# Gated attention heads finished in pairs: values, row sums and gates in groups, with the order of two projection tiles and of the gate matmuls changed

## The chip, the cores and the metric

The kernel runs on one core of one Trainium2 chip. The metric is the device time of one execution in microseconds. Before the change the median of three runs is 1924.27 us (1922.54 to 1924.54).

## What is computed

The reference is a two-layer encoder trunk on 512 tokens of width 1024:

```
for l in range(2):
    x = x + 0.5 * swiglu(rmsnorm(x))                   # feed-forward, 1024 -> 2816 -> 1024
    proj = rmsnorm(x) @ w_in                           # q,k,v | gq,gk,gv,gr | two gate codes
    na  = rmsnorm(neighbourhood_attention(q, k, v))    # 8 heads of 64
    gla = rmsnorm(o_fwd + o_bwd) * silu(gr)            # 4 gated linear-attention heads, dv = 128
    x = x + concat(na, gla) @ w_out
    x = x + 0.5 * swiglu(rmsnorm(x))
return rmsnorm(x)
```

A gated head has queries and keys of 64 and values of 128. Its forget gate comes from a rank-16 code, `log_sigmoid(code @ w_gate + b) / 16`, once for each direction. The head's output is divided by its root mean square, multiplied by a gain and by `silu(gr)`.

## The kernel before

All data is float32. Large products are made of three matmuls on float32r halves (`mm3`, line 182): the high part of the weights with both parts of the input, the low part with the high part. Between the two feed-forward stages of a layer stands `mixer` (line 583). It is the stage that the change touches; it runs twice.

The mixer has four streams of work, each a Python generator: the two pairs of gated heads (`gla_all(0)`, `gla_all(1)`, line 1036), the neighbourhood attention (`na_all`, line 969), and the filler (`fillers`, line 997), which makes the projection tiles of `win` in the order of `PAIRS` (line 39) and then multiplies by `w_out`. `interleave` (line 529) decides the order in which the streams are written. Each generator yields a pair (cost, delay): the planner adds the cost to its own clock and lets the stream go on no sooner than the delay after that. A yield of a name waits until the name stands in `got`. In each round the planner lets all streams that are due take steps in the order pair 0, neighbourhood attention, pair 1; then it runs what the last round left in `pend` (the transposes of gated values, line 772); then it takes filler steps for 5.3 units (`SLOT`). A filler step of a projection tile is six matmuls at 1.36 units.

TensorE's instructions are pinned to the order of writing while `interleave` runs (line 120). The orders of ScalarE and VectorE are chosen at compile time by a scheduler that plays the program through; they then run strictly in that order, each instruction waiting for its inputs.

PSUM has eight banks: four of tag `mm`, two of tag `sc`, one `tp` and one `o`. A bank can be written again only when every reader of its last content is done.

The parts that the change touches:

- `gla_gates` (line 611) makes the two gate tiles of a pair, one for each direction `d`. A gate tile is two matmuls into a bank, a ScalarE Abs and a VectorE minimum (line 622) that read the bank, and a chain after them. Pair 0 uses the `sc` banks; pair 1 uses `o` for the first direction and `tp` for the second, one directly behind the other.
- `gla_out` (line 797) ends one head. It waits for the head's `silu(gr)` (name `gs`) and transposed values (`gv`), issues 16 matmuls into an `mm` bank, squares and copies the result on ScalarE, and yields 3.6. Then `rsqrt_ms` (line 245) sums the squares over the partitions by two matmuls into `tp` (first head of a pair) or `sc` (second head). The row is read from the bank by two ScalarE instructions, Ln (line 261) and Identity (line 264); Exp (line 262) and three VectorE instructions follow. Two products on VectorE and `osplit` (line 794) give the parts `oh` that the output product needs.
- `rsqrt_ms` is also called once for the neighbourhood heads (line 989), into `tp`. The transposes of the attention probabilities (line 948) and of the gated values go through `tp` too.
- The filler's last part waits for the outputs of the heads, multiplies the neighbourhood half of `w_out` (eight chunks, `op_part(c, 0, 4)`) and half of the gated half for four chunks. What is left (`op_part(c, 6, 2)` and `op_part(c, 4, 4)`, line 1058) is done behind `interleave`; the profile calls that stage OP. Its weights come through two raw buffers and six split buffers.

In the rows, names that begin with M_ are tiles of the mixer, OP_ of the output stage, F_ of the feed-forward; M_sqh and M_sql are the two halves of a row sum's input, M_gr the gate value, M_gv the transposed values, M_pp the attention probabilities, M_mn the minimum of line 622, M_am the copies of the 128-wide scores.

Of the kernel before, what the change touches and what calls it, by code (L numbers as in the profile page):

```python
# [9 lines left out]
F32 = mybir.dt.float32  # L10
F32R = mybir.dt.float32r
U8 = mybir.dt.uint8
AF = mybir.ActivationFunctionType
ALU = mybir.AluOpType

P = 128
# [10 lines left out]
FAL = 1.4  # L27
HEAD = 9
MMB = 4
GOT = ('mm', 'mm')  # L30
WARM = 13
NAP = 4.0
SLOT = 5.3
# [10 lines left out]
         ('gk1', 'gq1'),  # L44
         ('q3', 'k3'),
         ('v2', 'v3'),
         ('gr0', 'gr1'),
         ('gv2', 'gv3'),
         ('gv0', 'gv1'),
         ('gr2', 'gr3'))  # L50
COLS = {"q": 0, "k": 512, "v": 1024, "gq": 1536, "gk": 1792, "gv": 2048, "gr": 2560}
TAGS = {'sl': 12, 'g0': 8, 'g1': 8, 'na': 6, 'ws': 5}
NPR = 12
NDF = 3
OPT = 2.56
OUTT = 3.6
GOTT = ('g0', 'g1')
# [3 lines left out]
def trunk_kernel(ctx, tc, xin, wgu, wdn, win, wcode, wgate, wout, vec, rpbt,  # L61
                 lmask, onesid, out, depth=DEPTH, stop=None):
    nc = tc.nc
    V, S, G, PE = nc.vector, nc.scalar, nc.gpsimd, nc.tensor
# [25 lines left out]
    def lvec(l, i):  # L90
        o = voff + l * 9 + i
        return vecs[:, o:o + 1]
# [4 lines left out]
    def nm(s):  # L97
        cnt[0] += 1
        return f"{st['lab']}_{s}_{cnt[0]}"

    def sl(name="s", dt=F32, tag="sl"):
        return sp.tile([P, T], dt, tag=tag, name=nm(name), bufs=TAGS[tag])

# [10 lines left out]
    def psum(tag):  # L114
        pool = {"mm": pm, "sc": ps2}.get(tag, ps1)
        return pool.tile([P, T], F32, tag=tag, name=nm(tag))

    def pinned(ins):

        if st.get("pin"):  # L120
            tc.keep_in_program_order(ins)
        return ins

    def MM(*args, **kw):
        return pinned(PE.matmul(*args, **kw))  # L125
# [30 lines left out]
    def split(src, h, l, gain=None):  # L156
        if gain is None:
            S.activation(h, src, AF.Copy)  # L158
            V.tensor_tensor(l, src, h.bitcast(F32), op=ALU.subtract)  # L159
        else:  # L160
            S.activation(h, src, AF.Copy, scale=gain)
            V.scalar_tensor_tensor(l, src, gain, h.bitcast(F32), ALU.mult, ALU.subtract)
# [79 lines left out]
    def lnexp():  # L242
        tc.keep_in_program_order(S.preload_act_table_set("natural_log_exp_and_others"))

    def rsqrt_ms(src, n, load=False, tag="sl", bank="tp"):
        if load:
            lnexp()
        ps = psum(bank)
        if tag == "sl":
            MM(ps, ones, src, start=True, stop=True)  # L250
        else:
            h, l = sl("sqh", F32R, tag), sl("sql", F32R, tag)
            split(src, h, l)
            MM(ps, onr, h, start=True, stop=False)
            MM(ps, onr, l, start=False, stop=True)

        return rsqrt_row(ps, n, *(sl(k, F32, tag) for k in ("ms", "r", "a")), act=tag != "sl")

    def rsqrt_row(ps, n, t, r, a, act=False):

        S.activation(r, ps, AF.Ln, bias=epsc, scale=1.0 / n)
        S.activation(r, r, AF.Exp, scale=-0.5)
        if act:
            S.activation(t, ps, AF.Identity, bias=epsc, scale=1.0 / n)
        else:
            V.tensor_scalar(t, ps, 1.0 / n, EPS, ALU.mult, ALU.add)
        V.tensor_tensor(a, r, r, op=ALU.mult)
        V.scalar_tensor_tensor(a, a, -0.5, t, ALU.mult, ALU.mult)  # L268
        V.scalar_tensor_tensor(r, a, 1.5, r, ALU.add, ALU.mult)
        return r  # L270
# [306 lines left out]
    def seq_out(a):  # L577
        return a.rearrange("p (r u c) -> p u r c", r=8, u=8)

    def unit_in(a):  # L580
        return a.rearrange("p (u r c) -> p u r c", u=8, r=8)

    def mixer(l):
        st["lab"] = f"M{l}"
        got = {}
# [23 lines left out]
        gla = [{}, {}]  # L609

        def gla_gates(pr):
            g = gla[pr]
            for d in range(2):
                gs, pk = sl("gs", F32, f"g{pr}"), sl("pk", F32, f"g{pr}")
                pg = psum("sc" if pr == 0 else ("o", "tp")[d])
                cs = slice(d * 256 + pr * P, d * 256 + (pr + 1) * P)
                MM(pg, wgh[:, cs], cr, start=True, stop=False)
                MM(pg, wgl[:64, cs], cr[:64], start=False, stop=True)
                b = lvec(l, 5 + 2 * d + pr)
                ab, mn = sl("ab", F32, "ws"), sl("mn", F32, "ws")  # L620
                S.activation(ab, pg, AF.Abs, bias=b)
                V.tensor_scalar(mn, pg, b, 0.0, ALU.add, ALU.min)
                S.activation(ab, ab, AF.Exp, scale=-1.0)
                S.activation(ab, ab, AF.Ln, bias=1.0)
                V.tensor_tensor(gs, mn, ab, op=ALU.subtract)
                prev = gs
                for h in (2, 4, 8, 16, 32, 64, 128):
                    n = T // h
                    cur = pk[:, GOFF[h]:GOFF[h] + n]
                    pv = prev.rearrange("p (b two) -> p two b", two=2)  # L630
                    V.tensor_tensor(cur, pv[:, 0, :], pv[:, 1, :], op=ALU.add)
                    prev = cur
                S.activation(gs, gs, AF.Exp, scale=1.0 / 16.0)
                S.activation(pk[:, :508], pk[:, :508], AF.Exp, scale=1.0 / 16.0)
                g["t1", d], g["tp", d] = gs, pk
# [11 lines left out]

        def gla_levels(pr):
            g = gla[pr]
            gla_gates(pr)  # L650
            yield 1.8, 6.0
            yield ("gq", pr)
            qa, ka = got["gq", pr], got["gk", pr]
# [5 lines left out]
            at = g["at"] = []  # L659
# [35 lines left out]
            for li, h in enumerate((1, 2, 4, 8, 16, 32, 64, 128)):  # L695
# [45 lines left out]
                elif h2 == 128:  # L741
                    pss = psum("sc"), psum("sc")
                    mms = []
                    for s in range(4):
                        t = s ^ 1
# [8 lines left out]
                else:  # L754
                    for half in range(2):
                        pss = psum("sc"), psum("sc")
                        kk, qq = (KF, QF) if half == 0 else (KB, QB)
                        o = 256 * (1 - half)
# [35 lines left out]
        def osplit(src, k, gain):  # L794
            ohl[k] = pair("oh", gain, src)

        def gla_out(hd, tag):
            g = gla[hd // 2]
            hh = hd % 2
            yield ("gs", hd)  # L800
            yield ("gv", hd)
            po = psum(tag)
            v = got["gv", hd]

            def vs(s):
                return v[:, s * P:(s + 1) * P]

            for t in range(4):
                dst = po[:, t * P:(t + 1) * P]
                half = 1 - t // 2  # L810
                fa = g["f", hh, half]
                s1 = t ^ 1
                MM(dst, vs(t), g["at"][hh][:, t * P:(t + 1) * P], start=True, stop=False)
                MM(dst, vs(s1), g["m", hh][:, s1 * P:(s1 + 1) * P], start=False, stop=False)
                for j in range(2):
                    o = j * 256 + (t % 2) * P
                    MM(dst, vs(2 * half + j), fa[:, o:o + P], start=False, stop=(j == 1))
            tag = GOTT[hd // 2]
            on, sq = sl("on", F32, tag), sl("sq", F32, tag)
            S.activation(sq, po, AF.Square)  # L820
            S.activation(on, po, AF.Copy, scale=0.125)
            got["po", hd] = True
            yield OUTT, 1.0
            r = rsqrt_ms(sq, 64 * P, False, tag, ("tp", "sc")[hh])
            V.tensor_tensor(on, on, r, op=ALU.mult)
            gp = got["gr", hd]
            V.tensor_tensor(unit_in(gp), seq_out(on), unit_in(gp), op=ALU.mult)
            osplit(gp, 4 + hd, lvec(l, 4))
            got["oh", hd] = True
            yield 0.9, 0.0  # L830


        def vmat_steps(src, done):
# [163 lines left out]
        def fillers():  # L997
            for i, (a, b) in enumerate(PAIRS):
                if i == 0:
                    continue  # L1000

                def done(j, ps):
                    turn = posts[a](j, ps, st["s"])
                    if turn:
                        pend.append(turn)

                steps = vmat_steps if a in ("v0", "v2") else tile_steps
                yield from steps(win[l, i], done)

            yield ("na",)  # L1010
            for c in range(KD):
                op_part(c, 0, 4)
                o = sl("on", F32, "ws")
                V.tensor_tensor(o, pss[c], got["na"], op=ALU.mult)  # L1014
                V.tensor_tensor(xt[:, c, :], xt[:, c, :], o, op=ALU.add)
                yield OPT, 0.0
            for hd in (1, 3):
                yield ("po", hd)
            yield ("oh", 0)
            yield ("oh", 1)  # L1020
            for c in range(MMB):
                op_part(c, 4, 2)
                yield 1.28, 0.0
# [11 lines left out]

        def gla_all(pr):
            yield from gla_levels(pr)
            for hd in (2 * pr, 2 * pr + 1):
                yield from gla_out(hd, GOT[pr])

        raw, ws = st.pop("dpre", (None, None))
        b0 = dmat(win[l, 0], ("mm", "mm"), raw, ws)
        r = stage_row()
# [25 lines left out]
    for c in range(KD):  # L1069
        xsplit(c, 0)  # L1070
        if c % 2 == 0:
            h, l = wnew()
# [147 lines left out]
```

## Time and profile before

| what | value |
|---|---|
| median of three runs | 1924.27 us |
| the profiled execution's own time | 1924.05 us |
| its span in the trace | 1922.3 us |
| VectorE busy | 1407.5 us (73%) |
| ScalarE busy | 1034.9 us (54%) |
| 16 DMA engines | 98 GB/s on average |
| chain that ended last | TensorE 91%, VectorE 4%, ScalarE 3% |

The time outside the span is 1.75 us. A busy TensorE means that a matmul is in the array; an instruction that waits at the head of its queue shows as idle time with the one that released it in brackets. Matmuls overlap by about half a duration, so issue distances are read from start to start.

### The profile page before, as it was taken

The page shows a single profiled execution, that of the slowest core. Times are in us where ns is not written, and L with a number is a line of the kernel's source. Part 1 is how long each engine was busy: PE and PEld are TensorE (multiplying, and loading weights), DVE is VectorE, ACT ScalarE, POOL GpSimd, SP SyncE. Part 2 cuts the span into 40 slices and gives each one's busy share as a digit, 9 for nine tenths or more (in the row PEclk, how much of TensorE's full clock was granted, in tenths as well). Part 3 has the DMA queues.
Part 4 walks back from the last instruction along what each step waited for, and adds up shares of the span by engine and source line. Part 5 has one row for each costly group of instructions (what it writes and reads, how often), then busy time and mean ns, then how long its engine had stood idle before and what let it go on. Part 6 is the DMA issues. An engine that isn't in the chain of part 4 may idle for free.

```text
span 1922.3 us, 32197 instructions
## 1 busy us (share of the span) xinstructions
PE 1897.2 (99%) x12490; PEld 1674.1 (87%) x12490; DVE 1407.5 (73%) x2695; ACT 1034.9 (54%) x1978; POOL 17.3 (1%) x36
## 2 busy tenths in 40 slices
PE   9999999999999999999999999999999999999997
PEld 8889989877887898989889899997887878999896
DVE  7958768676648976958787596776765689678585
ACT  6535536475765553635555264455666655446264
POOL 0000000000000000000000000000000000000000
PEclk9999999999999999999999999999999999999999
DMA  5332223322113233322332332232221133323322
GB/s 179 107 106 100 95 103 127 113 78 78 61 48 101 94 107 108 110 100 93 102 101 91 109 110 101 98 121 96 89 89 56 39 115 110 110 88 111 110 78 77
DMA packets 58249, 187.78 MB, mean 98 GB/s; under 512 B 6640, under 2 KB 13296, under 8 KB 45808
## 3 DMA queue, kind: packets, MB, share of 16 engines
q1 hardware_dynamic: 30480, 133.12, 20.2%
q10 hardware_dynamic: 25056, 44.22, 7.0%
q0 software_dynamic: 2560, 8.39, 1.4%
q8 instruction: 98, 1.61, 0.3%
q14 instruction: 55, 0.45, 0.1%
HBM read 183.60 MB, written 2.10 MB: 97 GB/s over the span
## 4 chain that ended last, share of the span: by engine, by line
PE 91%; DVE 4%; ACT 3%; issue 1%; DMA 1%; ACTq 0%; DVEq 0%
PE F_mm L125 42%; PE F_sc L125 27%; PE M_mm L125 14%; PE M_sc L125 2%; PE F_tp L125 1%; PE F_o L125 1%; PE M_tp L128 1%; PE M_o L125 1%; PE OP_mm L125 1%; PE M_tp L125 1%; DVE M_on L1014 0%; DVE OP_wl L159 0%; PE I_o L125 0%; DMA OP_wraw<-in_wgu 0%; DVE M_a L268 0%
## 5 line engine op out<-in xcount | busy, mean ns | idle before, releaser
L125 PE MATMUL F_mm<-F_xc,F_wh 128*128 128x256 f32 x3584 | 638.3, 282 | 1.7 <-ACT F_o L310 1.2
L125 PEld LDWEIGHTS F_mm<-F_xc,F_wh 128*128 128x128 f32 x3584 | 553.8, 190 | 5.7 <-ACT F_o L310 1.5
L158 ACT ACTIVATE F_wh<-F_wraw 128x512 fp32r<-128x512 f32 (+1 forms) x472 | 289.0, 617 | 435.1 <-PE F_sc L125 240.5
L125 PE MATMUL F_mm<-F_xc,F_wl 128*128 128x256 f32 x1792 | 496.6, 282 | 0.0
L125 PE MATMUL F_sc<-F_hid,F_wh 128*128 128x512 f32 (+1 forms) x1432 | 438.8, 387 | 1.3 <-DVE xt L479 1.3
L159 DVE TENSOR_TENSOR F_wl<-F_wraw,F_wh 128x512 fp32r<-128x512 f32 (+1 forms) x472 | 313.4, 670 | 147.4 <-ACT F_wh L158 141.1
L125 PEld LDWEIGHTS F_mm<-F_xc,F_wl 128*128 128x128 f32 x1792 | 336.4, 190 | 0.0
L125 PEld LDWEIGHTS F_sc<-F_hid,F_wh 128*128 128x128 f32 x1432 | 265.7, 188 | 54.6 <-DVE xt L479 3.0
L125 PE MATMUL F_sc<-F_hid,F_wl 128*128 128x512 f32 (+1 forms) x716 | 276.7, 386 | 0.0
L158 ACT ACTIVATE F_wh<-F_ws 128x512 fp32r<-128x512 f32 x256 | 161.6, 632 | 165.1 <-PE F_mm L125 104.7
L159 DVE TENSOR_TENSOR F_wl<-F_ws,F_wh 128x512 fp32r<-128x512 f32 x256 | 174.9, 689 | 39.2 <-ACT F_wh L158 36.4
L125 PE MATMUL M_mm<-F_xd,M_wh 128*128 128x512 f32 x608 | 193.7, 399 | 0.0
L125 PEld LDWEIGHTS F_sc<-F_hid,F_wl 128*128 128x128 f32 x716 | 134.6, 188 | 26.5
L479 DVE SCALAR_TENSOR_TENSOR xt<-F_sc,xt 128x512 f32<-128x512 f32 x94 | 65.0, 691 | 96.8 <-PE F_sc L125 96.2
L125 PEld LDWEIGHTS M_mm<-F_xd,M_wh 128*128 128x128 f32 x608 | 112.4, 189 | 24.7 <-issue 1.9
L159 DVE TENSOR_TENSOR M_wl<-M_wraw,M_wh 128x512 fp32r<-128x512 f32 (+1 forms) x112 | 74.2, 669 | 62.3 <-ACT M_wh L158 44.0
L125 PE MATMUL M_mm<-F_xd,M_wl 128*128 128x512 f32 x304 | 119.5, 393 | 0.0
L158 ACT ACTIVATE M_wh<-M_wraw 128x512 fp32r<-128x512 f32 (+1 forms) x112 | 67.9, 616 | 67.8 <-PE M_mm L125 48.8
L125 PEld LDWEIGHTS M_mm<-F_xd,M_wl 128*128 128x128 f32 x304 | 57.4, 189 | 12.5
L125 PE MATMUL F_mm<-OP_xd,F_wh 128*128 128x512 f32 x224 | 67.4, 390 | 0.0
L159 DVE TENSOR_TENSOR F_hid<-F_o,F_hid 128x512 fp32r<-128x512 f32 x88 | 60.4, 689 | 1.3
L158 ACT ACTIVATE F_hid<-F_o 128x512 fp32r<-128x512 f32 x88 | 54.7, 625 | 5.2 <-DVE F_o L414 3.8
(298 smaller groups left out, 2645.7 us busy)
## 6 DMA issues: line engine op xcount, KB each, us to landing
F_wraw<-in_wgu SPq DMA_DIRECT2D x64, 1024.0 KB, 4.8
F_wraw<-in_wdn SPq DMA_DIRECT2D x32, 1024.0 KB, 4.9
M_wraw<-in_win ACTq DMA_DIRECT2D x88, 256.0 KB, 3.6
F_wraw<-in_wgu ACTq DMA_DIRECT2D x76, 256.0 KB, 3.7
F_wraw<-in_wdn SPq DMA_DIRECT2D x16, 768.0 KB, 4.2
M_pp<-in_rpbt POOLq DMA_DIRECT2D x32, 256.0 KB, 3.5
M_wraw<-in_wout SPq DMA_DIRECT2D x16, 256.0 KB, 2.7
xt<-in_xin SPq DMA_DIRECT2D x8, 256.0 KB, 5.2
```

Source lines behind the costliest of these rows:

```text
L125: return pinned(PE.matmul(*args, **kw))
L128: return pinned(PE.transpose(*args))
L158: S.activation(h, src, AF.Copy)
L159: V.tensor_tensor(l, src, h.bitcast(F32), op=ALU.subtract)
L479: V.scalar_tensor_tensor(xt[:, c, :], pss[j], 0.5, xt[:, c, :], ALU.mult, ALU.add)
```

## The change

Four edits:

1. In `PAIRS` the values of heads 0 and 1 (`gv0`, `gv1`) move ahead of `gr0`, `gr1`; the values of heads 2 and 3 stay second of these four entries.
2. Pair 1's second gate tile is written 0.9 units later with a delay of 3.0 units, and both tiles of pair 1 use bank `o`.
3. `gla_out` becomes `gla_heads`, which ends both heads of a pair together: the value matmuls, square and copy of both heads (each as soon as its `gv` is there), then both row sums with the product by the reciprocal root, then, when `gs` is there, both gate products and splits. The wait for `gs` stands behind the row sums. Tag `g0` gets nine buffers instead of eight.
4. The filler waits for all four `po` instead of those of heads 1 and 3.

```
-         ('gr0', 'gr1'),
-         ('gv2', 'gv3'),
-         ('gv0', 'gv1'),
+         ('gv0', 'gv1'),
+         ('gv2', 'gv3'),
+         ('gr0', 'gr1'),
          ('gr2', 'gr3'))
-TAGS = {'sl': 12, 'g0': 8, ...}
+TAGS = {'sl': 12, 'g0': 9, ...}

         def gla_gates(pr):
             for d in range(2):
...
-                pg = psum("sc" if pr == 0 else ("o", "tp")[d])
+                if pr and d:
+                    yield 0.9, 3.0
+                pg = psum("o" if pr else "sc")

+        def gla_heads(pr):
+            g = gla[pr]
+            tag = GOTT[pr]
+            heads = []
+            for hh, hd in enumerate((2 * pr, 2 * pr + 1)):
+                yield ("gv", hd)
+                po = psum("mm")
...
+                on, sq = sl("on", F32, tag), sl("sq", F32, tag)
+                S.activation(sq, po, AF.Square)
+                S.activation(on, po, AF.Copy, scale=0.125)
+                got["po", hd] = True
+                heads.append((hd, on, sq))
+                yield OUTT / 2, 0.0
+            yield 0.0, 1.0
+            for hh, (hd, on, sq) in enumerate(heads):
+                r = rsqrt_ms(sq, 64 * P, False, tag, ("tp", "sc")[hh])
+                V.tensor_tensor(on, on, r, op=ALU.mult)
+                yield 0.5, 0.0
+            for hd, on, sq in heads:
+                yield ("gs", hd)
+                gp = got["gr", hd]
+                V.tensor_tensor(unit_in(gp), seq_out(on), unit_in(gp), op=ALU.mult)
+                osplit(gp, 4 + hd, lvec(l, 4))
+                got["oh", hd] = True

-            for hd in (1, 3):
+            for hd in range(4):
                 yield ("po", hd)
```

## Rows read from the trace of the kernel before

**Rows 1.** The page's first part, TensorE.

```profile
PE 1897.2 (99%) x12490; PEld 1674.1 (87%) x12490; DVE 1407.5 (73%) x2695; ACT 1034.9 (54%) x1978; POOL 17.3 (1%) x36
```

**Rows 2.** Waits of TensorE, whole span: us in total, times, longest us.

```profile
PE M_tp L128 <- DVE M_mn L622: 3.2, 2, 1.6
PE OP_mm L125 <- DVE OP_wl L159: 2.3, 2, 1.1
PE OP_mm L125 <- ACT OP_wh L158: 1.8, 3, 0.8
...
PE M_sc L125 <- ACT M_am L752: 1.3, 1, 1.3
...
PE OP_mm L125 <- DVE xt L1063: 0.6, 2, 0.3
...
PE M_mm L125 <- ACT M_oh L161: 0.2, 1, 0.2
```

**Rows 3.** Timeline, TensorE around pair 1's gates: start, length, instructions, idle before.

```profile
386.33 0.51 PE L125 MATMUL M_o<-M_cr,wgh 128*128 128x512 f32 x1
...
387.19 0.50 PE L125 MATMUL M_tp<-M_cr,wgh 128*128 128x512 f32 x1
...
393.73 0.69 PE L125 MATMUL M_sc<-M_gkq,M_gkq 64*64 64x64 f32 x32
396.05 0.66 PE L128 MATMUL M_tp<-con,M_pp 128*128 128x128 f32 x4 [1.62 <-DVE M_mn L622]
```

**Rows 4.** Timeline, VectorE in the same stretch.

```profile
390.40 0.74 DVE L622 TENSOR_SCALAR M_mn<-M_o,vecs 128x512 f32<-128x512 f32 x1
...
393.29 0.61 DVE L943 TENSOR_SCALAR M_pp<-M_pp,M_sm 128x256 f32<-128x256 f32 x2
...
395.25 0.74 DVE L622 TENSOR_SCALAR M_mn<-M_tp,vecs 128x512 f32<-128x512 f32 x1
```

**Rows 5.** Timeline, TensorE around the first row sums.

```profile
543.11 0.39 PE L125 MATMUL M_mm<-F_xd,M_wl 128*128 128x512 f32 x1
...
552.84 0.39 PE L125 MATMUL M_tp<-M_sqh,onr 128*128 128x512 f32 x1
...
553.31 0.38 PE L125 MATMUL M_mm<-M_at,M_gv 128*128 128x128 f32 x2
...
556.80 0.48 PE L125 MATMUL M_tp<-M_sqh,onr 128*128 128x512 f32 x1
```

**Rows 6.** Timeline, ScalarE behind the first row sum.

```profile
553.46 1.28 ACT L261 ACT_TABLE_LOAD   x1
554.75 0.69 ACT L261 ACTIVATE M_r<-M_tp,vecs 128x512 f32<-128x512 f32 x1
555.34 0.68 ACT L264 ACTIVATE M_ms<-M_tp,vecs 128x512 f32<-128x512 f32 x1
556.04 1.28 ACT L262 ACT_TABLE_LOAD   x1
```

**Rows 7.** Timeline, ScalarE behind the tile of gr2.

```profile
544.01 1.28 ACT L787 ACT_TABLE_LOAD   x1
545.30 0.63 ACT L787 ACTIVATE M_gr<-M_gr 128x512 f32<-128x512 f32 x1
```

**Rows 8.** Chain that ended last, 540 to 615 us: start, length, what.

```profile
595.49 0.73 ACT M_oh L161
...
597.62 2.54 DMA OP_wraw<-in_wgu
...
606.61 0.61 DVE OP_wl L159
...
609.92 0.64 ACT OP_wh L158
```

**Rows 9.** Windows, TensorE: stretch, us, busy (instructions), granted clock, DMA share, GB/s.

```profile
459.00:463.00 4.00, 2.56 (x43) 1.00 0.73 249
463.30:466.70 3.40, 3.40 (x9) 0.50 0.01 2
```

More of the change, by code (lines that the diff above doesn't have):

```diff
@@ L29 @@
 MMB = 4
-GOT = ('mm', 'mm')
 WARM = 13
@@ L46 @@
          ('v2', 'v3'),
+         ('gv0', 'gv1'),
+         ('gv2', 'gv3'),
          ('gr0', 'gr1'),
-         ('gv2', 'gv3'),
-         ('gv0', 'gv1'),
          ('gr2', 'gr3'))
 COLS = {"q": 0, "k": 512, "v": 1024, "gq": 1536, "gk": 1792, "gv": 2048, "gr": 2560}
-TAGS = {'sl': 12, 'g0': 8, 'g1': 8, 'na': 6, 'ws': 5}
+TAGS = {'sl': 12, 'g0': 9, 'g1': 8, 'na': 6, 'ws': 5}
 NPR = 12
@@ L649, in gla_levels @@
             g = gla[pr]
-            gla_gates(pr)
+            yield from gla_gates(pr)
             yield 1.8, 6.0
@@ L795, in osplit @@
             ohl[k] = pair("oh", gain, src)
[L797 to L830, printed above, removed]
@@ new lines, in gla_heads, with vs @@
+        def gla_heads(pr):
[5 more added lines that the diff above has]
+                po = psum("mm")
+                v = got["gv", hd]
+                def vs(s):
+                    return v[:, s * P:(s + 1) * P]
+                for t in range(4):
+                    dst = po[:, t * P:(t + 1) * P]
+                    half = 1 - t // 2
+                    fa = g["f", hh, half]
+                    s1 = t ^ 1
+                    MM(dst, vs(t), g["at"][hh][:, t * P:(t + 1) * P], start=True, stop=False)
+                    MM(dst, vs(s1), g["m", hh][:, s1 * P:(s1 + 1) * P], start=False, stop=False)
+                    for j in range(2):
+                        o = j * 256 + (t % 2) * P
+                        MM(dst, vs(2 * half + j), fa[:, o:o + P], start=False, stop=(j == 1))
+                on, sq = sl("on", F32, tag), sl("sq", F32, tag)
[15 more added lines that the diff above has]
+                got["oh", hd] = True
@@ L1037, in gla_all @@
             yield from gla_levels(pr)
-            for hd in (2 * pr, 2 * pr + 1):
-                yield from gla_out(hd, GOT[pr])
+            yield from gla_heads(pr)
         raw, ws = st.pop("dpre", (None, None))
```

## The prediction

> **What bounds the kernel now.** I read the busy times first, then TensorE's waits, then its timeline where the change lies. TensorE is busy for 1897.2 of 1922.3 us [rows 1], so it is the bound and no other engine's work counts unless TensorE stops for it. The change moves TensorE's matmuls and adds or removes none. What it can be worth is therefore what it adds to or takes from the waits at the head of TensorE's queue. In the two mixers and the output stages behind them these waits are few [rows 2]: twice 1.6 us for the bank of a gate tile, once 1.3 us for a ScalarE copy (layer 0), 2.3 + 1.8 us for output weights, 0.6 and 0.2 us for the banks and the last head of that stage. They add up to 9.4 us, so some 4.7 us a mixer can be won at most, and every new wait is paid in full.
>
> Which waits are new follows from the planner's arithmetic (cost and delay of each yield, rounds of 5.3 units). Stepped through for the kernel before, it gives head 0's values, a gv transpose, filler, row sum 0 into `tp`, head 1's values, the neighbourhood row sum into `tp`, head 2's values and output chunks; the trace has the middle of this in the same order [rows 5]. Stepped through for the changed kernel it gives, in the parts that matter:
>
> - pair 1's first gate tile in `o`, four filler steps, pair 0's first scores, the first attention transpose in `tp`, and only then the second gate tile in `o`;
> - tile gr0 done, one filler step of gr1, **row sum 0 (`tp`), row sum 1 (`sc`), an attention transpose (`tp`), pair 1's scores (both `sc`)**, with nothing between;
> - tile gr3 done, **neighbourhood row sum (`tp`), row sum 2 (`tp`), row sum 3 (`sc`)**, with nothing between, then all eight output chunks of the neighbourhood half, the four half chunks, and the output stage.
>
> **The change part by part**, for one mixer. All lengths come from one profiled execution, whose own time, 1924.05 us, lies 0.2 us under the median.
>
> *Gates through one bank.* Now the transpose waits 1.62 us for the minimum that reads the second gate tile in `tp` [rows 3], which VectorE starts only at 395.25 [rows 4]. In the new order `tp` is free there. What is late next is the transpose's own input: the probabilities are done at 393.29 + 0.61 = 393.90 [rows 4]. A gate tile takes 387.19 - 386.33 = 0.86 us of TensorE [rows 3] and moves behind the transpose, so the transpose is reached at 396.05 - 1.62 - 0.86 = 393.57 and waits about 0.4 us. The gain is 1.62 - 0.4 = 1.2 us. The ends are 1.62 (the probabilities come early too) and 0.8 (VectorE gives them up later). The new wait that this adds, second gate tile for the reader of the first in the same `o`, costs nothing: that reader ran at 390.40 [rows 4], over 3 us ahead of the matmul; behind it stands filler, which would be delayed if it were late.
>
> *Row sums 0 and 1, then a transpose.* Take t as the end of tile gr0. Two 512-column matmuls take 553.31 - 552.84 = 0.47 us [rows 5], so six take 1.4. Row sum 0 is issued at t + 1.4, row sum 1 at t + 1.9, and the transpose is reached at t + 2.35. It must wait until Ln and Identity have read row sum 0 out of `tp`. ScalarE has its own business then: silu of gr0, which is ready once VectorE has scaled the tile. The same situation is in the trace of before at tile gr2: its last matmul is issued at 543.11, so t is 543.33; the silu table load starts at 544.01 and the silu ends at 545.30 + 0.63 = 545.93, that is t + 2.6 [rows 5, 7]. The scheduler pulled that silu ahead of everything it could. Then Ln needs a table load again, and from the start of that load to the end of Identity the trace has 555.34 + 0.68 - 553.46 = 2.56 us [rows 6]. `tp` is free at t + 5.2 and the transpose waits 2.8 us. Row sum 1 needs Ln and Identity as well, 0.6 us each from start to start, which frees `sc` at t + 6.4; the scores get there 0.66 us [rows 3] behind the transpose's start, at t + 5.8, and wait 0.55 us. Sum: 3.4 us. If Ln comes ahead of silu, without a load, it starts when the second matmul has drained (0.39 us long, issued 0.235 apart), t + 2.05, Identity ends at t + 3.3, the transpose waits 0.95 us and the scores 0.55 us: 1.5 us. I take 3.4, because in rows 7 silu starts its load 0.7 us behind the tile's end and row sum 0 is only done 2.05 us behind it.
>
> The Trainium skill, "ScalarE: Activation LUTs", section "Table sets: the hidden batching unit", says to batch activations by set, and that Ln followed by Exp needs one load, since one set has both. The first half speaks against this change: it brings Ln between two silus. On the second half the trace differs: Ln loads at 553.46 and Exp loads again at 556.04 [rows 6]. By the page Exp's second load would be absent, which comes behind the readers of the bank and changes no wait above. The same page's section "What ACT_TABLE_LOAD costs" adds a drain of about 1.38 us to each load, which would make the 3.4 us some 6.2, an estimate; the row of 1.28 us is followed by Ln after 1.29 us, so here the measurement decides.
>
> *Neighbourhood row sum, then row sum 2.* Now head 1's values stand between two uses of `tp`: row sum 0 at 552.84, the neighbourhood's at 556.80 [rows 5], and Identity frees the bank at 555.34 + 0.68 = 556.02 [rows 6], just in time. The change takes that cover away. From issue to free is 556.02 - 552.84 = 3.2 us, with one table load because a silu went before; the second row sum is reached 0.47 us after the first: a wait of 2.7 us. The situation is the same (a last gr tile just ended, its first silu long done), so I take this. The lower end, with no load and Ln at once, is 0.47 + 0.2 + 1.27 - 0.47 = 1.5 us; the upper end, with the last silu and its load in front of it (1.28 + 0.63 us, rows 7), is 4.6 us. Behind row sum 2 are row sum 3 and the output chunks, and all of them move by the wait.
>
> *Earlier end of the heads.* In the chain that ended last the output stage hangs on the last head: oh of head 3 at 595.49, then weights, a load into a freed raw buffer at 597.62, a split at 606.61 and one at 609.92 [rows 8]. In the new order eight output chunks of twelve matmuls (2.8 us each by the 0.235 us above) stand between the row sums and the output stage, so all of that chain's first part is over, and chunks 0 to 3 end one by one, not in a burst. I take off (2.3 + 1.8 + 0.2) / 2 = 2.1 us [rows 2]. The lower end is nothing, if the weights' loads alone set the pace (2.54 us for one [rows 8]); it can't be a loss, as less stands in front of the same work. The upper end is 2.4, with the 0.6 us for the banks.
>
> *Without a cost in the sum.* The value transpose of head 1 now follows an attention transpose in `tp` with only the 32 small score matmuls between: 0.66 + 0.69 us [rows 3] cover one ScalarE read of 0.69 [rows 6]; the upper end is a table load in front of it, 1.28 us. Values of heads 0 and 1 take an extra `mm` bank between projection tiles; if the pool gives the bank of the tile just ended, the next tile waits for its reader, one VectorE instruction of some 0.7 us and its way there: 0 to 1.3 us, taken at 0, as the banks of the head and of the attention scores are free by then; there is no such wait now, so nothing to win. The ninth buffer and the wait for four `po` change no order.
>
> Sum for one mixer: 3.4 + 2.7 - 1.2 - 2.1 = +2.8 us. Two mixers: +5.6 us, 1929.7 us against the execution's 1924.05; against the median **1930**.
>
> **The rivals.**
>
> *The waits are short.* If ScalarE reads the row sums at once and without a load, the sum is 1.5 + 1.5 - 1.2 - 2.1 = -0.3 us a mixer: 1923.7. For it: nothing but the scheduler's choice puts silu first. Against it: rows 6 and 7, where table loads stand in both places. It decides at the start of Ln: less than 0.3 us behind the second matmul of its row sum.
>
> *It gets faster.* With short waits, the gate's full 1.6 us, and the output stage's 2.4, it is 1.5 + 1.5 - 1.6 - 2.4 = -1.0 a mixer. If also the 1.3 us for the copies of layer 0 [rows 2] go, and with them the stretch at half clock that follows them, 3.4 us at 1.2 GHz, half of it lost [rows 9], that is another -3.0: 1919.3. For it: in layer 1 neither is there. Against it: the change doesn't touch that place, only what ScalarE does before it.
>
> *The clock falls too.* TensorE's granted clock was 0.50 (1.2 GHz) from 463.3 to 466.7 us, after it had been busy for 2.56 of 4 us [rows 9]; that cost 1.7 us. The four new long waits are longer than the one there. If each is followed by such a stretch, it is 1930 + 4 x 1.7 = 1937. Against it: the wait of 1.62 us [rows 3] is followed by none.
>
> **How the numbers follow.** 0.45 for the forecast, 0.27 for short waits, 0.18 for faster, 0.10 for the clock. A change under 0.2% (3.85 us) can't be told from none here: slower is above 1928.1, faster below 1920.4. Slower: the forecast and the clock, less 0.02 of the forecast that ends lower, 0.53; same: 0.27; faster: 0.20. The forecast's own range is 1926 to 1934. The range for 8 in 10 reaches from 1920, where most of the short waits and half of the faster case lie above, to 1937.
>
> **What would show it.** Right: TensorE idle for 2 to 3 us ahead of row sum 2 and ahead of a transpose of M_pp, both released by the Identity of line 264; no wait for M_mn; less than 1 us of waits in the output stage. Wrong: row sums released within 1.5 us, no table load ahead of Ln, or an output stage that waits as long as now.

## The result, and the profile after

The changed kernel takes 1956.48 us (median of four runs, 1955.67 to 1956.87) against 1923.95 us before in the same comparison: 1.017 times as long, 95% interval 1.0152 to 1.0187. The way was forecast, the size was not: +32.5 us instead of +6. The first part of the page of the changed kernel:

```profile
PE 1905.8 (98%) x12490; PEld 1680.6 (86%) x12490; DVE 1409.8 (72%) x2695; ACT 1045.2 (53%) x1984; POOL 17.3 (1%) x36
```

The span grew by 32.3 us, TensorE's busy time only by 8.6, with the same 12490 matmuls [rows 1]. The difference is waiting. TensorE's waits in the changed kernel (us in total, times, longest us):

```profile
PE M_sc L124 <- ACT M_sqh L157: 24.8, 4, 6.8
PE M_tp L124 <- ACT M_ms L263: 5.2, 2, 2.6
PE M_o L124 <- ACT M_vm L889: 2.4, 4, 0.8
PE M_sc L124 <- ACT M_am L754: 1.4, 1, 1.4
```

Against [rows 2], the waits for M_mn (gates) and for output weights are gone, and a wait is there that I had not seen coming: four times the second row sum of a pair waits for its own input, M_sqh. TensorE's timeline at pair 0 of layer 0, and then at the neighbourhood row sum and pair 1, where before stood [rows 5]:

```profile
533.35 0.61 PE L124 MATMUL M_mm<-F_xd,M_wh 128*128 128x512 f32 x2
...
534.71 0.39 PE L124 MATMUL M_tp<-M_sqh,onr 128*128 128x512 f32 x1
534.95 0.40 PE L124 MATMUL M_tp<-M_sql,onr 128*128 128x512 f32 x1
540.99 0.80 PE L124 MATMUL M_sc<-M_sqh,onr 128*128 128x512 f32 x1 [5.64 <-ACT M_sqh L157]
541.79 0.80 PE L124 MATMUL M_sc<-M_sql,onr 128*128 128x512 f32 x1
542.39 1.05 PE L127 MATMUL M_tp<-con,M_pp 128*128 128x128 f32 x4
...
572.85 0.39 PE L124 MATMUL M_tp<-M_sqh,onr 128*128 128x512 f32 x1
...
576.08 0.50 PE L124 MATMUL M_tp<-M_sqh,onr 128*128 128x512 f32 x1 [2.60 <-ACT M_ms L263]
...
583.57 0.79 PE L124 MATMUL M_sc<-M_sqh,onr 128*128 128x512 f32 x1 [6.76 <-ACT M_sqh L157]
```

The order is the one that the planner's arithmetic gave. What ScalarE does meanwhile (same kernel, its timeline):

```profile
526.29 0.60 ACT L823 ACTIVATE M_sq<-M_mm 128x512 f32<-128x512 f32 x1 [3.32 <-PE M_mm L124]
...
532.64 1.31 ACT L157 ACTIVATE M_wh<-M_wraw 128x512 fp32r<-128x512 f32 x2 [2.21 <-PE M_mm L124]
533.97 1.28 ACT L789 ACT_TABLE_LOAD   x1
535.26 0.63 ACT L789 ACTIVATE M_gr<-M_gr 128x512 f32<-128x512 f32 x1
535.91 1.28 ACT L260 ACT_TABLE_LOAD   x1
537.21 0.69 ACT L260 ACTIVATE M_r<-M_tp,vecs 128x512 f32<-128x512 f32 x1
537.79 0.68 ACT L263 ACTIVATE M_ms<-M_tp,vecs 128x512 f32<-128x512 f32 x1
538.49 1.28 ACT L261 ACT_TABLE_LOAD   x1
539.78 0.63 ACT L261 ACTIVATE M_r<-M_r 128x512 f32<-128x512 f32 x1
540.32 0.61 ACT L157 ACTIVATE M_sqh<-M_sq 128x512 fp32r<-128x512 f32 x1
```

The square of head 1 is done at 526.29 + 0.60 = 526.89, 13.4 us ahead of its split (540.32), and ScalarE stood idle for 2.21 us in between. So the split did not wait for its data or for the engine at first; it came only behind silu and behind Ln, Identity and Exp of head 0, with the three table loads of these. TensorE's clock falls within these waits, too. Windows over the four stretches at a lowered clock (us, busy us and matmuls, granted clock, DMA):

```profile
539.40:549.60 10.20, 8.25 (x24) 0.50 0.00 0
577.00:587.20 10.20, 3.61 (x8) 0.50 0.01 3
1505.40:1512.20 6.80, 4.52 (x14) 0.50 0.00 0
1542.90:1553.10 10.20, 4.95 (x11) 0.50 0.00 0
sum 37.40, PE 21.33; mean PE 5.33
```

The granted clock there is 0.50 (1.2 GHz). TensorE was busy for 21.3 us of them, so half of that, some 10.7 us, was lost. Before it was one stretch of 3.4 us [rows 9], which is gone here; TensorE's busy time grew by about the difference, 8.6 us.

Together, over both mixers: 24.8 + 5.2 us of waits and 10.7 us of clock are new, 40.7 us; 3.2 us of gate waits, 4.7 us of output-stage waits (2.3 + 1.8 + 0.6) and 1.7 us of the old stretch are gone, 9.6 us. That is +31.1 us of the +32.3. Another 1.1 us stands at the waits for M_vm (2.4 against 1.3 us in all): in each mixer one of them grew from 0.24 to 0.75 us.

### The profile page after: what moved, and what is told of

It reads as the page before. It is cut to its first block, busy times and chain, and to the rows that moved or that the text cites. A ratio compares the mean times of both kernels' runs of the same rounds, so it can differ in the third digit from the quotient of the medians.

```text
span 1954.6 us, 32205 instructions
## 1 busy us (share of the span) xinstructions
PE 1905.8 (98%) x12490; PEld 1680.6 (86%) x12490; DVE 1409.8 (72%) x2695; ACT 1045.2 (53%) x1984; POOL 17.3 (1%) x36
## 4 chain that ended last, share of the span: by engine, by line
PE 94%; ACT 4%; DVE 2%; issue 0%; ACTq 0%; DVEq 0%
PE F_mm L124 42%; PE F_sc L124 27%; PE M_mm L124 18%; PE M_sc L124 2%; PE F_tp L124 1%; PE F_o L124 1%; PE OP_mm L124 1%; PE M_tp L127 1%; PE M_o L124 1%; PE M_tp L124 1%; ACT L261 0%; PE I_o L124 0%; DVE M_wl L158 0%; ACT L789 0%; ACT L260 0%
```

## The experiments

My theory at this point was: M_sqh of the second head has to wait for a buffer. A pair's temporaries share the nine (g0) or eight (g1) buffers of one tag. At the second split, `on` of both heads, the square of the second, the split of the first and Ln's, Identity's and the product's tiles of the first hold eight. The second split asks for two more, M_sqh and M_sql, and none of the eight comes free before the first row sum's matmuls are done. By this count g1 has no buffer left and g0 one, so the count alone does not say why M_sqh waits in g0 too. The rivals: ScalarE is late because of its table loads, or the scheduler prefers the first head's chain, whatever the buffers; or the order of the tiles is the cause.

### Parts alone

**The gates alone** (the kernel before with the second edit):

```
-                pg = psum("sc" if pr == 0 else ("o", "tp")[d])
+                if pr and d:
+                    yield 0.9, 3.0
+                pg = psum("o" if pr else "sc")
...
-            gla_gates(pr)
+            yield from gla_gates(pr)
```

> The kernel before with the second edit alone (second gate tile of pair 1 later, both in bank o). If the edits are independent and the loss is all in the grouped heads: the 1.6 us wait of the first attention transpose goes in each mixer, about -1.5 us twice, 1921 us. If the gates' edit has a part in the loss: 1924 or more, with a wait in the row sums.

Measured: 1920.96 us, 0.999 times the time of before (0.9981 to 0.9998). The wait for M_mn (3.2 us) is gone, the other waits of [rows 2] stand nearly as they were, and the waits for M_vm grow by the same 1.1 us as in the changed kernel: 2.1 us are left, near the 2.2 us measured. The edit is good by itself, and has no part in the loss.

**The order of PAIRS alone** (the kernel before with the first edit):

```
-         ('gr0', 'gr1'),
+         ('gv0', 'gv1'),
          ('gv2', 'gv3'),
-         ('gv0', 'gv1'),
+         ('gr0', 'gr1'),
```

> The kernel before with the new order of PAIRS alone, heads still ended one by one and still waiting for silu(gr) first. If grouping is the cause: no wait for M_sqh, within 2 us of 1924. If pulling the gated values ahead is the cause: row sums and silus meet here too, waits of some us ahead of a row sum and over 1935 us.

Measured: 1925.88 us, 1.0015 (1.0006 to 1.0024). New is a wait of 1.4 us for M_sql in each mixer. No wait for M_sqh: the order is not the cause alone.

**The grouped heads alone** (the changed kernel with gates and order as before):

```
-         ('gv0', 'gv1'),
+         ('gr0', 'gr1'),
          ('gv2', 'gv3'),
-         ('gr0', 'gr1'),
+         ('gv0', 'gv1'),
...
-                if pr and d:
-                    yield 0.9, 3.0
-                pg = psum("o" if pr else "sc")
+                pg = psum("sc" if pr == 0 else ("o", "tp")[d])
```

> The changed kernel with the gates' edit and the order of PAIRS undone, so the grouped heads (with nine buffers in g0) alone. If grouping is the cause: the wait of the second row sum for its split M_sqh stands in both pairs, 5 to 7 us each, and the time is 1950 to 1960 us. If the cause is the order of the projection tiles: under 1935 us.

Measured: 1941.16 us, 1.0096 (1.0081 to 1.0112). The waits for M_sqh are there four times, but 9.6 us in all, 2.4 at most, with 4.8 us of waits for Identity. Neither of my numbers: grouping costs some 18 us, and by subtraction 14 more come only when order and grouping meet. In that order row sums 0 and 1 stand beside the silu of gr0; that this is the reason is not shown.

### Buffers or ScalarE

**Both splits ahead of the first row sum** (the changed kernel):

```
...
+            parts = []
+            for hd, on, sq in heads:
+                parts.append((sl("sqh", F32R, tag), sl("sql", F32R, tag)))
+                split(sq, *parts[-1])
             for hh, (hd, on, sq) in enumerate(heads):
-                r = rsqrt_ms(sq, 64 * P, False, tag, ("tp", "sc")[hh])
+                r = rsqrt_ms(sq, 64 * P, False, tag, ("tp", "sc")[hh], parts[hh])
```

> The changed kernel, but both heads' squares are split into M_sqh and M_sql ahead of the first row sum, so that the buffers of the two splits are taken before those of the first row sum's Ln, Identity and product. Everything else as in the changed kernel. Theory (the second split has to wait for a buffer that the first row sum's matmuls give back, and then stands behind Ln, Exp and their table loads on ScalarE): the waits of 5.6 and 6.8 us for M_sqh go, and with them most of the half clock behind them; waits for Identity stay or come (2.6 us ahead of row sum 2, some 3 us behind row sum 1): 1928 to 1934 us. Rival (ScalarE is late because of the silu table loads, whatever the buffers): the second row sum is as late as before, over 1948 us.

Measured: 1944.67 us, 1.0112 (1.0098 to 1.0126). The wait for M_sqh is gone (the second split now starts at 528.08), but only 11.8 us were won, less than the theory's number needs and more than the rival's allows: waits for Identity stand in its place (5.7 + 5.5 + 5.2 us). This edit also changes the order of writing, so it does not tell a buffer from a preference of the scheduler.

**Other buffers, same order** (the changed kernel; M_sqh and M_sql of the second head from tag sl):

```
...
-            h, l = sl("sqh", F32R, tag), sl("sql", F32R, tag)
+            h, l = sl("sqh", F32R, own or tag), sl("sql", F32R, own or tag)
...
-                r = rsqrt_ms(sq, 64 * P, False, tag, ("tp", "sc")[hh])
+                r = rsqrt_ms(sq, 64 * P, False, tag, ("tp", "sc")[hh], (None, "sl")[hh])
```

> The changed kernel with nothing moved: only M_sqh and M_sql of a pair's second head take their buffers from tag sl (twelve) instead of g0 and g1. The order of writing, and with it the scheduler's preference for Ln, Identity and Exp of the first row sum, is that of the changed kernel, unlike in e4. If buffers are what the second split waits for: M_sqh is written ahead of the first row sum, its waits of 24.8 us go, and the run looks as e4, 1938 to 1946 us, with waits for Identity instead. If the preference on ScalarE is the cause: M_sqh stands behind Exp as before, over 1950 us.

Measured: 1946.26 us, 1.0115 (1.0100 to 1.0131). Its waits:

```profile
PE M_tp L124 <- ACT M_ms L263: 6.2, 2, 3.1
PE M_sc L124 <- ACT M_ms L263: 5.5, 2, 3.2
PE M_tp L127 <- ACT M_ms L263: 5.4, 2, 2.7
```

M_sqh does not appear (M_sql does, with 0.6 us), and on ScalarE the split of pair 0's second head now comes ahead of silu, Ln and Exp:

```profile
534.40 1.31 ACT L157 ACTIVATE M_wh<-M_wraw 128x512 fp32r<-128x512 f32 x2 [2.21 <-PE M_mm L124]
535.62 0.61 ACT L157 ACTIVATE M_sqh<-M_sq 128x512 fp32r<-128x512 f32 x1
536.25 1.28 ACT L789 ACT_TABLE_LOAD   x1
```

Nothing but the buffers was changed, so the buffers were what put the second split behind silu, Ln and Exp. It still starts 7 us behind its square, later than with the splits first; what it waits for there is not shown. What the buffers cost is some 10 us of the 32.5. The other 22 are the banks' readers, which were hidden behind that wait (17.1 us of waits for Identity, in the rows above), and the clock: the slow stretches that are not in the kernel before have 18.1 us of TensorE's busy time, half of it lost, 9 us. The gates and the output stage give some 6 us back.

**No silu** (the changed kernel; the gate value is copied, so the output lacks silu):

```
-                    S.activation(got["gr", hd], got["gr", hd], AF.Silu)
+                    S.activation(got["gr", hd], got["gr", hd], AF.Copy)
```

> The changed kernel with silu(gr) left out (a copy in its place), so that ScalarE never leaves the table set of Ln and Exp in the mixer. Theory in two parts (the second split waits for a buffer of the first row sum, and the table loads of 1.28 us around it make the wait long): the wait for M_sqh shrinks to the length of Ln, Identity, Exp and the split, 2 to 3 us, the wait for Identity ahead of row sum 2 to 1.5 us, and little half clock is left: 1928 to 1936 us. If buffers alone set it: over 1948 us. If tables alone set it: no M_sqh wait over 1 us, under 1925 us.

Measured: 1943.46 us, 1.0104 (1.0088 to 1.0119). The waits:

```profile
PE M_sc L124 <- ACT M_sqh L157: 12.6, 4, 3.9
PE M_tp L124 <- ACT M_ms L263: 2.7, 2, 1.4
```

Both are half of what they were, and the loads at Ln and Exp (six each in the changed kernel) are gone: ScalarE's table loads double the price of each wait. The total was expected lower than it came, and none of the three numbers is right; four stretches at half clock remain beside these waits, three of 6.83 us and one of 3.41, and the old one of 3.4 us is back.

### Where the row sums stand

**Row sums of pair 1 in other banks** (on top of the splits first):

```
-("tp", "sc")[hh], parts[hh])
+(("tp", "sc"), ("o", "sc"))[pr][hh], parts[hh])
```

> Splits first as in e4, and the row sums of pair 1 in banks o and sc instead of tp and sc, so that row sum 2 has not to wait for the neighbourhood row sum's readers. If the wait of 2.6 us for Identity there is paid in full, with the 3.4 us at half clock behind it: e4 less 2.6 to 4.3 us a mixer, 1936 to 1939 us. If the wait is only moved to the output chunks behind it: 1943 to 1945 us.

Measured: 1946.72 us, 1.0117 (1.0103 to 1.0131). The wait of 2.6 us ahead of row sum 2 is gone, and the output stage now waits 4.0 us for OP_wh, the output weights' split on ScalarE, and 1.8 us for OP_wl on VectorE, with stretches at half clock there (6.83 us from 616.0, 3.41 us from 1578.5): the second number of the expectation, or a little above. Against the splits first, where the output stage waits 1.6 us for OP_wh, 4.2 of the 5.2 us that TensorE no longer waits ahead of row sum 2 come back there.

**silu waited for first, nothing else** (the changed kernel):

```
+            for hd in (2 * pr, 2 * pr + 1):
+                yield ("gs", hd)
             yield 0.0, 1.0
             for hh, (hd, on, sq) in enumerate(heads):
...
             for hd, on, sq in heads:
-                yield ("gs", hd)
```

> The changed kernel with the wait for silu(gr) put back ahead of the row sums and nothing else. Banks are asked for late enough in this order; what is left is the buffer that the second split has to wait for. If buffers are a cause of their own: waits for M_sqh of 2 to 5 us in both pairs, 1925 to 1936 us. If the place of the row sums was all: as e7, 1915 to 1919 us.

Measured: 1947.48 us, 1.0124 (1.0111 to 1.0138). Row sums at pair 0 in its timeline:

```profile
551.36 0.39 PE L124 MATMUL M_tp<-M_sqh,onr 128*128 128x512 f32 x1
557.68 0.79 PE L124 MATMUL M_sc<-M_sqh,onr 128*128 128x512 f32 x1 [5.69 <-ACT M_sqh L157]
```

The place of the row sums is another, no reader of a row sum's bank is waited for any more, and the second row sum waits 5.7 us for its split as before (22.3 us in all). The wait for the split does not need the banks' readers; that it is a matter of buffers in this place too was not tried by itself. It is above my range since the waits are longer than 5 us and since there is half clock again, 6.8 us at each of the four.

**The same with splits first and other banks**:

```
+            for hd in (2 * pr, 2 * pr + 1):
+                yield ("gs", hd)
             yield 0.0, 1.0
             parts = []
...
-("tp", "sc")[hh], parts[hh])
+(("tp", "mm"), ("o", "sc"))[pr][hh], parts[hh])
```

> Splits first, row sums in tp and mm (pair 0) and o and sc (pair 1), and the wait for silu(gr) put back ahead of the row sums. By the planner's arithmetic row sums 0 and 1 then stand two tiles later, ahead of the values of heads 2 and 3, and row sums 2 and 3 behind three output chunks. If the cause is that a row sum's input and bank are asked for sooner than ScalarE can give them: no wait over 1 us is left in the heads, the gates' 1.5 us and some 2 us of the output stage are won in each mixer: 1915 to 1919 us. If grouping itself costs: over 1924 us.

Measured: 1935.78 us, 1.0064 (1.0051 to 1.0077). No wait is left at the row sums, but the kernel is still 12.7 us over the one before:

```profile
PE M_mm L124 <- DVE M_on L1029: 5.4, 8, 1.1
PE OP_mm L124 <- DVE xt L1077: 4.9, 2, 2.5
```

VectorE reads the output chunks' banks too late. My first number was wrong: with the waits of the heads gone, grouping still costs. That fits the two heads' chains falling on VectorE and ScalarE at once while the output chunks want them, but I have not tried that by itself.

### What else could be had

**Gates and order, with a later row sum** (heads one by one):

```
-            yield OUTT, 1.0
+            yield OUTT, 4.0
```

> The kernel before with the gates' edit and the new order of PAIRS, heads one by one, and the delay ahead of a head's row sum 4.0 instead of 1.0 units. If the cost of the order alone (waits of 1.4 us for M_sql in each mixer) comes from row sums asked for too soon: no wait for M_sql, at or under the gates alone, 1918 to 1921 us. If the order costs in another way: 1922 to 1925 us.

Measured: 1924.58 us, 1.0006 (0.9997 to 1.0014), so no different from before. The waits for M_sql are unchanged at 2.9 us, and the row sums stand in the same places as with the order alone. So the longer delay moved nothing, the run does not try the theory, and the cause of the order's cost stays open.

**Buffers, and the table set loaded by name** (on top of the other buffers):

```
             yield 0.0, 1.0
+            lnexp()
             for hh, (hd, on, sq) in enumerate(heads):
```

> e9 with the table set that holds both Ln and Exp loaded by name ahead of each pair's row sums, so that Ln and Exp of both heads need no further load. If the table loads between the two heads' rows (Exp's and the second Ln's, 2.56 us) make the wait of the second scores: it falls from 2.3 to 3.2 us to under 1 us, the waits for Identity of the transpose and of row sum 2 stay (2.7 us each), and less half clock follows: 1934 to 1941 us. If the named load is placed elsewhere or the silus undo it: within 3 us of e9's 1946.

Measured: 1951.27 us, 1.0146 (1.0131 to 1.0162): 5 us above the run before it and outside both numbers. In its trace Ln and Exp of both heads of pair 0 still each load a table of their own; no load by name stands beside them. Why it is slower is open, and the run says nothing on the theory.

**Gates alone, and the table set loaded by name ahead of each head's row sum**:

```
-            r = rsqrt_ms(sq, 64 * P, False, tag, ("tp", "sc")[hh])
+            r = rsqrt_ms(sq, 64 * P, True, tag, ("tp", "sc")[hh])
```

> The gates' edit alone (e1) with the same named load ahead of each head's row sum. If table loads in the last heads' chain are what makes the output weights late: 1 to 3 us off the waits of the output stage, 1916 to 1920 us. If those waits hang on the loads of the weights: as e1, 1921 us.

Measured: 1916.52 us, 0.9966 (0.9953 to 0.9978): faster than both kernels, and some 4 us under the gates alone. ScalarE behind row sum 0, where before stood [rows 6]:

```profile
552.94 1.28 ACT L243 ACT_TABLE_LOAD   x1
554.23 0.69 ACT L261 ACTIVATE M_r<-M_tp,vecs 128x512 f32<-128x512 f32 x1
554.82 0.68 ACT L264 ACTIVATE M_ms<-M_tp,vecs 128x512 f32<-128x512 f32 x1
555.51 1.28 ACT L789 ACT_TABLE_LOAD   x1
556.81 0.63 ACT L789 ACTIVATE M_gr<-M_gr 128x512 f32<-128x512 f32 x1
557.46 1.28 ACT L243 ACT_TABLE_LOAD   x1
558.75 0.63 ACT L262 ACTIVATE M_r<-M_r 128x512 f32<-128x512 f32 x1
559.29 0.67 ACT L261 ACTIVATE M_r<-M_tp,vecs 128x512 f32<-128x512 f32 x1
...
561.38 0.65 ACT L262 ACTIVATE M_r<-M_r 128x512 f32<-128x512 f32 x1
```

The loads at Ln and Exp of their own (lines 261 and 262, two each in the gates alone) are gone; at the row sums only those by name (line 243, 16 instead of 10) and silu's are left. So there are two loads more in all, not fewer; what is saved is one load around row sum 0. TensorE's waits for output weights fall from 2.3 + 1.8 us [rows 2] to

```profile
PE OP_mm L125 <- ACT OP_wh L158: 1.5, 2, 0.8
...
PE OP_mm L125 <- DVE OP_wl L159: 0.6, 2, 0.3
```

So 2.0 us of the waits for output weights hang on where ScalarE's table loads stand. That it is the last heads' chain is not shown: the load saved is at head 0, and head 3's Ln has a load ahead of it that the gates alone do not have. Nor do these waits make up the whole gain.

## Why the prediction was right in its way and wrong in its size

*Gates: right.* 1.2 us a mixer was forecast. In the changed kernel the scores and the transpose stand almost together, where before 1.62 us of waiting lay between them [rows 3]:

```profile
393.04 0.69 PE L124 MATMUL M_sc<-M_gkq,M_gkq 64*64 64x64 f32 x32
393.86 0.65 PE L127 MATMUL M_tp<-con,M_pp 128*128 128x128 f32 x4
```

The transpose starts 393.86 - 393.04 - 0.69 = 0.13 us behind the scores' end instead of the 0.4 us forecast, so 1.5 us are won. Of these 0.5 us are lost again at the wait for M_vm, for which the prediction had no term. The gates alone won 2.2 us in two mixers.

*Row sums 0 and 1: the step that failed.* Its first half held to a tenth: silu first, a table load, Ln, Identity, and `tp` free at t + 5.2. The trace has the tile's end at 533.35 and Identity's at 537.79 + 0.68 = 538.47, t + 5.1. But the prediction then let row sum 1 be issued at t + 1.9, with its input there, and called the ninth buffer an edit that changes no order. It was issued at t + 7.6, as its split waited for a buffer. I had named the tag's buffers and not counted them: eight tiles are held where the second split asks for two more. In place of 3.4 us stood 5.6 us at pair 0, and at pair 1, where I had no term at all for row sum 3, 6.8 us. The waits for the banks' readers that I did forecast came out as soon as the buffers were there: in the run with other buffers the transpose waits 2.7 us (forecast 2.8), row sum 2 waits 3.1 (2.7), and the scores 2.3 to 3.2 (0.55). The last one was short because I put Ln of head 1 right behind Identity of head 0; in the trace Exp and two table loads come between. So a second part of the step failed too, and more buffers alone would not have brought the forecast: with them the kernel is still 23 us over the one before, not 6, by the longer waits for the scores and by the clock.

*Neighbourhood row sum, then row sum 2: right.* 2.7 us forecast, 2.60 measured, released by the Identity of line 264 (263 in the changed kernel) as said.

*Output stage: right in its number, not shown in its cause.* 2.1 us a mixer forecast; all 4.7 us of waits in two mixers are gone. But TensorE also stands still for some 15 us in each mixer ahead of that stage, in which the other engines can catch up. Where the row sums' waits are gone (the last run under "Where the row sums stand"), the output stage waits 6.8 us for OP_wh, OP_wl and xt, more than before. The earlier end of the heads by itself has not been shown to win anything; that the number came out may be luck.

*The clock: the rival happened.* I gave it 0.10, since the wait of 1.62 us [rows 3] is followed by no slow stretch, and the sum had nothing for it. The four waits of 5.6 to 6.8 us have one each: the slow stretches begin within the waits (539.4 in one from 535.4 to 541.0) and last for 6.8 or 10.2 us. They cost 10.7 us, where the rival had 4 x 1.7. The old slow stretch stood behind a wait of only 1.3 us [rows 2, 9], and the gates alone have a wait of that length in the same place without it (TensorE's timeline, then the window around it):

```profile
460.65 1.37 PE L125 MATMUL M_sc<-M_ga,M_gkq 64*64 64x64 f32 x32 [1.37 <-ACT M_am L754]
...
455.00:475.00 20.00, 18.51 (x191) 1.00 0.25 80
```

So the length of one wait does not tell by itself whether the clock falls, and that the old stretch is gone from the changed kernel's trace need not be the change's doing.

*The signs.* The wait ahead of row sum 2, the missing wait for M_mn and the quiet output stage came. The wait ahead of a transpose of M_pp did not: the transpose stands behind row sum 1's 5.6 us, and waits only in the run with other buffers.

*The waits are short*, and *it gets faster*: both wrong, for the reason that rows 6 and 7 gave against them.

## What to carry to other kernels

Where work of two units is grouped, count the tiles of each tag that are alive at every point of the new order, in the order of allocation; a pool that was enough for one unit at a time can make the group serial again, and an order that is pinned on the busiest engine turns this into idle time. A wait on an engine that switches tables is paid with the loads that the scheduler put in front, so read what stands between the producer and the consumer in its queue. Try the parts of a bundle one by one: here the gates alone won time, and the sum lost it.

## What the runs showed of the hardware

With Ln and Exp on the table that the build chooses for each, each loads its own: 1.28 us twice for one row [rows 6]. Loaded by name, one table serves both: in the last run Exp, the next Ln and the next Exp (558.75, 559.29, 561.38) follow one load at 557.46. The loads by name are the one edit between the kernels of 1916.5 us and 1921.0 us. The Trainium skill, "ScalarE: Activation LUTs", section "Table sets: the hidden batching unit", says that one set has both, and the last run agrees; that the two are loaded one by one if nothing names the set is what the traces add. In all the rows shown here a load is followed by its first instruction after 1.29 to 1.30 us.

At the lowered clock the same 512-column matmul's row shows 0.80 us instead of 0.40 us (M_sql at 541.79 against 534.95 us in the changed kernel).
